# Scaling the normed tokens ahead of the transposition instead of inside it, in a two-layer encoder trunk

## The chip, the core and the metric

The kernel runs on one core of a Trainium2 chip. The metric is the device time of one execution in microseconds (us). The engines named here are TensorE (PE, matrix products; PEld is its weight load), VectorE (DVE), ScalarE (ACT), GpSimd (POOL) and the sync engine's queue of transfers (SP). Each engine works through its own instructions in the order in which they were compiled; semaphores tie the engines together.

## The reference

`x` holds 512 tokens of 1024 features, all F32. Two layers follow, each a token mixer (retention, stick-breaking attention and gated linear attention on one input projection) and a convolutional FFN of width 2816. What matters here is what stands around every sub-layer:

```python
def rmsnorm(x, g):
    xf = x.astype(jnp.float32)
    y = xf * lax.rsqrt(jnp.mean(xf * xf, axis=-1, keepdims=True) + EPS)
    return (y * g.astype(jnp.float32)).astype(x.dtype)
...
        hn = rmsnorm(x, pre_mix_g[l]) * (1.0 + sc1) + sh1
        y = token_mixer(hn, w_in[l], gla_w2[l], gla_b[l], ret_norm_g[l], gla_norm_g[l], w_out[l])
        x = x + g1 * rmsnorm(y, post_mix_g[l])
        hn = rmsnorm(x, pre_ffn_g[l]) * (1.0 + sc2) + sh2
        y = conv_ffn(hn, w_up[l], conv_w[l], conv_b[l], w_down[l])
        x = x + g2 * rmsnorm(y, post_ffn_g[l])
```

So between any two sub-layers a residual is formed, normed, scaled and shifted, and it has to lie transposed (features on the partitions) for the next products.

## The kernel before, in words

The tokens are four blocks of 128, here block 0 to 3 (`tb` in the code). A block of the residual is two tiles of 128x512 F32 (`xt[0]`, `xt[1]`), with the tokens on the partitions. Every large product is done with three products of first and second parts: an operand is cast to a first part (`hi`, `hnh`; ScalarE, lines 352 and 332) and the rest is a second part (`lo`, `hnl`; VectorE, lines 353 and 333). All products of the program are recorded at line 92, and transpositions at line 95.

There are four places at which tokens are normed and transposed. At the start, `start_x` does it for the input. Three hand-overs follow: the first from the mixer to the FFN of layer 0 (about 353 to 390 us in the trace), the second from that FFN to the mixer of layer 1 (724 to 790 us), the third from the mixer to the FFN of layer 1 (1061 to 1100 us). The last FFN writes the output.

In a hand-over each block goes the same way. `close0` and `close1` square the two banks of the sub-layer's output on ScalarE (line 516, junk output, sum kept), multiply it by the gate's row on VectorE (518), and get 1/rms from two small VectorE operations (283, 284) and one on GpSimd (286). The old residual is loaded again by the sync queue (`load_x`), the sum is formed on VectorE (522), stored, squared on ScalarE (298, twice), and 1/rms of the sum is got in the same way. `scaled_ident` then multiplies the identity by it (304). `prenorm_T`, run when `flush` calls it, does four products of 128x128 into each of two PSUM banks, evicts the first bank in four pieces on ScalarE (328) and the second in four on VectorE (330), with the scale and shift of the next sub-layer, and makes the first and second parts (332, 333).

The two banks come from the `pj` pool of three banks. So the second bank of block 1 takes the bank that the first of block 0 had, and waits for its eviction, and the banks of block 2 wait in the same way for those of block 0 and of block 1. In the second hand-over the products of `sv` (lines 502 on, `proj_tok`, evicted at 544) share these banks. An FFN begins with the products of blocks 0 and 1 for four tiles of w_up (the lead products), goes on with those of blocks 2 and 3, and only then to whole rows of tokens.

Nothing orders the work around the change but the program: the compiler's scheduler sets each engine's order when the kernel is built, from the dependences and its own idea of durations. Transfers on the sync queue go in that order too; a load of a weight tile waits until the tile that had its slot has been split into its parts.

## Time and profile before

| | us |
|---|---|
| median of three runs | 1462.37 |
| lowest, highest | 1459.83, 1466.27 |
| profiled execution, span from first to last instruction | 1457.7 |
| PE busy in that span | 1409.9 (97%) |
| DVE, ACT, POOL busy | 832.6 (57%), 661.5 (45%), 36.1 (2%) |
| mean granted clock of TensorE | 0.976 |

The page gives the profiled execution's span alone; no time of its own stands beside it. The median lies 4.67 us above that span. A stretch in which PE is not busy, or runs at less than the full clock, adds to the time unless PE can do other work in it; the other engines have slack on average, but each in its order.

### The profile page before, as it was taken

What the parts mean: (1) busy time and instruction counts of PE and PEld (TensorE: products, weight loads), DVE (VectorE), ACT (ScalarE), POOL (GpSimd) and SP (SyncE); (2) the same over time, 40 slices, a digit from 0 to 9 for tenths busy, and PEclk for the clock granted to TensorE, in tenths of its full rate; (3) what the DMA queues carried; (4) which work ended last, traced back from release to release, by engine and by line L of the source; (5) the groups of instructions that cost most, each with busy time, mean ns of one, the idle gap of its engine ahead of it and who ended that gap; (6) DMA issues with size and microseconds to landing.
All of it is one profiled execution on the core that took longest, in us unless ns stands there. A gap on an engine that the chain in (4) does not pass through costs nothing. (4 is left out here: it accounts for less than half of the span.)

```text
span 1457.7 us, 19702 instructions
## 1 busy us (share of the span) xinstructions
PE 1409.9 (97%) x7619; PEld 1131.1 (78%) x7619; DVE 832.6 (57%) x1544; ACT 661.5 (45%) x1081; POOL 36.1 (2%) x57
## 2 busy tenths in 40 slices
PE   8999799999999999999989999999999999999998
PEld 6887476768878778888879877777789888888886
DVE  4459687655878784433654486576575444443232
ACT  5455366745533333332244565766564333333130
POOL 0000000000000000000010000000010000000000
PEclk9999799989999999999999999999899999999999
DMA  8635272203688772222773221022053222223222
GB/s 308 213 122 151 92 229 73 73 30 127 208 235 255 215 232 101 101 87 101 246 172 112 87 87 59 30 73 73 29 203 102 92 97 102 98 90 101 101 102 101
DMA packets 73614, 186.22 MB, mean 128 GB/s; under 512 B 8448, under 2 KB 9520, under 8 KB 73520
## 3 DMA queue, kind: packets, MB, share of 16 engines
q1 hardware_dynamic: 72512, 182.68, 38.8%
q0 software_dynamic: 704, 2.11, 0.5%
q8 instruction: 60, 0.98, 0.3%
q14 instruction: 34, 0.28, 0.1%
q10 hardware_dynamic: 304, 0.16, 0.0%
HBM read 176.51 MB, written 8.41 MB: 127 GB/s over the span
## 5 line engine op out<-in xcount | busy, mean ns | idle before, releaser
L353 DVE TENSOR_TENSOR lo<-raw,hi 128x1024 fp32r<-128x1024 f32 (+2 forms) x208 | 245.7, 1184 | 259.1 <-ACT hi L352 254.3
L92 PE MATMUL pj<-hnh,hi 128*128 128x512 f32 x976 | 385.8, 395 | 7.5 <-DVE m__867_4559 L914 3.3
L92 PE MATMUL pj<-hnh,lo 128*128 128x512 f32 x976 | 384.4, 394 | 0.0
L92 PE MATMUL pj<-hnl,hi 128*128 128x512 f32 x976 | 383.3, 393 | 0.0
L352 ACT CAST hi<-raw 128x1024 fp32r<-128x1024 f32 (+2 forms) x208 | 211.3, 1018 | 332.3 <-PE pj L92 170.6
L92 PEld LDWEIGHTS pj<-hnh,hi 128*128 128x128 f32 x976 | 184.8, 189 | 48.2 <-issue 8.9
L92 PEld LDWEIGHTS pj<-hnh,lo 128*128 128x128 f32 x976 | 184.5, 189 | 39.5 <-issue 1.1
L92 PEld LDWEIGHTS pj<-hnl,hi 128*128 128x128 f32 x976 | 184.7, 189 | 37.7 <-issue 0.2
L250 DVE SCALAR_TENSOR_TENSOR ada<-ada,cB 128x512 f32<-128x512 f32 x160 | 107.6, 688 | 40.6 <-DMA ada<-ada 40.2
L92 PE MATMUL pj<-hi,hnh 128*128 128x384 f32 (+1 forms) x160 | 52.2, 326 | 5.2 <-ACT m__1248_6605 L544 5.2
L92 PE MATMUL pj<-lo,hnh 128*128 128x384 f32 (+1 forms) x160 | 51.8, 324 | 0.3 <-DVE lo L353 0.3
L92 PE MATMUL pj<-hi,hnl 128*128 128x384 f32 (+1 forms) x160 | 51.7, 323 | 0.0
L286 POOL TENSOR_TENSOR s<-s,nhalf 128x1 f32<-128x1 f32 x32 | 20.0, 625 | 795.2 <-DVE s L284 790.5
L92 PE MATMUL ps<-hnl,hi 128*128 128x256 f32 x128 | 36.4, 288 | 1.1 <-DVE hnl L333 1.1
L92 PE MATMUL ps<-hnh,lo 128*128 128x256 f32 x128 | 36.0, 285 | 0.0
L92 PE MATMUL ps<-hnh,hi 128*128 128x256 f32 x128 | 35.8, 290 | 0.0
L92 PEld LDWEIGHTS pj<-hi,hnh 128*128 128x128 f32 x160 | 30.8, 192 | 5.8 <-ACT m__1248_6605 L544 5.4
L516 ACT ACTIVATE junk<-ps 128x512 bf16<-128x512 f32 x16 | 9.5, 596 | 50.8 <-PE ps L92 50.5
L92 PEld LDWEIGHTS pj<-lo,hnh 128*128 128x128 f32 x160 | 30.8, 192 | 0.9 <-DVE lo L353 0.7
L92 PEld LDWEIGHTS pj<-hi,hnl 128*128 128x128 f32 x160 | 30.7, 192 | 0.0
L92 PEld LDWEIGHTS ps<-hnl,hi 128*128 128x128 f32 x128 | 24.6, 194 | 1.6 <-DVE hnl L333 1.6
L92 PEld LDWEIGHTS ps<-hnh,hi 128*128 128x128 f32 x128 | 24.8, 198 | 0.0
(2770 smaller groups left out, 2536.2 us busy)
## 6 DMA issues: line engine op xcount, KB each, us to landing
raw<-wu SPq DMA_DIRECT2D x88, 512.0 KB, 3.3
ada<-ada SPq DMA_DIRECT2D x160, 256.0 KB, 3.5
raw<-wd SPq DMA_DIRECT2D x44, 512.0 KB, 3.2
raw<-wT SPq DMA_DIRECT2D x42, 512.0 KB, 3.6
raw<-wo SPq DMA_DIRECT2D x16, 512.0 KB, 3.2
raw<-wsv SPq DMA_DIRECT2D x8, 384.0 KB, 4.0
raw<-wrv SPq DMA_DIRECT2D x8, 384.0 KB, 2.9
raw<-wgv SPq DMA_DIRECT2D x8, 272.0 KB, 2.8
```

The costliest lines, as they stand in the source:

```text
L92: self.last = self.e.matmul(*a, **k)
L250: V.scalar_tensor_tensor(raw, raw, 1.0, cB[h], ALU.mult, ALU.mult, accum_out=pt[:, 4 * h + j : 4 * h + j + 1])
L286: G.tensor_tensor(r, v, nhalf, ALU.pow)
L352: SC.copy(h, raw)
L353: V.tensor_tensor(l_, raw, as32(h), ALU.subtract)
L516: SC.activation(junk, ps, AF.Square, accum_out=ss)
```

## The change

The pool of the diagonals and `scaled_ident` go. `scaled` takes their place: half of a block (128x512) is multiplied by 1/rms on VectorE, the other half on ScalarE. At the start it writes in place; in a hand-over it writes to two new tiles, as the unscaled residual is still being stored. TensorE then transposes the scaled tiles with the identity. Comments were taken out too, so that later lines have numbers that are lower by one.

```diff
-    dgp = ctx.enter_context(tc.tile_pool(name="dgp", bufs=2))
...
-    def scaled_ident(r):
-        # a product with the diagonal of 1 / rms both scales and transposes
-        dg = dgp.tile([P, P], F32, tag="dg", name=nm("dg"))
-        V.tensor_scalar(dg, ident, r, None, ALU.mult)
-        return dg
+    def scaled(xt, r, to):
+
+        V.tensor_scalar(to[0], xt[0], r, None, ALU.mult)
+        SC.activation(to[1], xt[1], AF.Copy, scale=r)
+        return to
 
     def prenorm(tb, xt, ft, a, sh, hi, lo):
         r = rstd_of(square_sums(xt))
-        dg = scaled_ident(r)
-        late[tb] = lambda: prenorm_T(tb, xt, dg, ft, a, sh, hi, lo)
+        xn = scaled(xt, r, [T(ft), T(ft)])
+        late[tb] = lambda: prenorm_T(tb, xn, ft, a, sh, hi, lo)
...
-    def prenorm_T(tb, xt, dg, ft, a, sh, hi, lo):
+    def prenorm_T(tb, xn, ft, a, sh, hi, lo):
         for h in range(2):
             ps = psj()
             for j in range(4):
-                PE.matmul(ps[:, j * P : j * P + P], xt[h][:, j * P : j * P + P], dg, start=True, stop=True)
+                PE.transpose(ps[:, j * P : j * P + P], xn[h][:, j * P : j * P + P], ident)
...
     def start_x(tb):
         cs = slice(tb * P, tb * P + P)
-        dg = scaled_ident(rstd_of(square_sums(xt0[tb])))
+        xn = scaled(xt0[tb], rstd_of(square_sums(xt0[tb])), xt0[tb])
         for h in range(2):
             ps = (psz, psj)[h]()
             for j in range(4):
-                PE.matmul(ps[:, j * P : j * P + P], xt0[tb][h][:, j * P : j * P + P], dg, start=True, stop=True)
+                PE.transpose(ps[:, j * P : j * P + P], xn[h][:, j * P : j * P + P], ident)
```

The order of the instructions on ScalarE and VectorE moves in the hand-overs. ScalarE in the third hand-over, before: `m__1780` is block 0's first bank being evicted, `m__1771` and `m__1772` are block 2's residual (its squares), `m__1797` is block 1's first bank and `m__1815` block 2's; the squares of block 3 follow further down.

```order
L328 ACTIVATE m__1780_9393<-pj_1779_9388,mod1sh2_5617,A12_9267 128x128 x4
L352 CAST hi_1804_9498<-raw_1803_9496 128x1024
L332 CAST hnh_1746_9265<-m__1780_9393 128x512
L298 ACTIVATE junk_112,s_1774_9377<-m__1771_9368 128x512
L332 CAST hnh_1746_9265<-m__1782_9405 128x512
L352 CAST hi_1807_9504<-raw_1806_9502 128x1024
L298 ACTIVATE junk_112,s_1775_9378<-m__1772_9369 128x512
L516 ACTIVATE junk_112,s_1784_9437<-ps_1783_9412 128x512
L352 CAST hi_1810_9510<-raw_1809_9508 128x1024
L328 ACTIVATE m__1797_9471<-pj_1796_9466,mod1sh2_5617,A12_9267 128x128 x4
L328 ACTIVATE m__1815_9569<-pj_1814_9564,mod1sh2_5617,A12_9267 128x128
L332 CAST hnh_1746_9265<-m__1797_9471 128x512
```

ScalarE at the same place, after: `m__1778` is block 2's residual, `m__1785` its scaled half, `m__1787` block 0's first bank; `m__1795` and `m__1796` are block 3's residual, `m__1803` its scaled half, `m__1805` block 1's first bank.

```order
L297 ACTIVATE junk_109,s_1781_9395<-m__1778_9386 128x512
L515 ACTIVATE junk_109,s_1791_9456<-ps_1790_9431 128x512
L303 ACTIVATE m__1785_9404<-m__1778_9386,s_1783_9401 128x512
L327 ACTIVATE m__1787_9412<-pj_1786_9407,mod1sh2_5622,A12_9280 128x128 x4
L351 CAST hi_1818_9531<-raw_1817_9529 128x1024
L331 CAST hnh_1750_9278<-m__1787_9412 128x512
L331 CAST hnh_1750_9278<-m__1789_9424 128x512
L351 CAST hi_1839_9801<-raw_1838_9799 128x1024
L297 ACTIVATE junk_109,s_1798_9474<-m__1795_9465 128x512
L297 ACTIVATE junk_109,s_1799_9475<-m__1796_9466 128x512
L303 ACTIVATE m__1803_9484<-m__1796_9466,s_1801_9481 128x512
L327 ACTIVATE m__1805_9492<-pj_1804_9487,mod1sh2_5622,A12_9280 128x128 x4
```

Block 0's eviction moved from ahead of block 2's squares to behind block 2's scaling, and block 1's from ahead of block 3's squares to behind block 3's scaling.

VectorE in the third hand-over, before: `dg_1778` is block 2's diagonal, `m__1799` block 1's second bank, `m__1788` and `m__1789` block 3's residual.

```order
L283 TENSOR_TENSOR s_1776_9381<-s_1774_9377,s_1775_9378 128x1
L284 TENSOR_SCALAR s_1776_9381<-s_1776_9381 128x1
L304 TENSOR_SCALAR dg_1778_9386<-ident_95,s_1777_9384 128x128
L518 TENSOR_TENSOR m__1785_9439<-ps_1783_9412,g1_1_9056 128x512
L283 TENSOR_TENSOR s_1786_9441<-s_1724_9194,s_1784_9437 128x1
L284 TENSOR_SCALAR s_1786_9441<-s_1786_9441 128x1
L353 TENSOR_TENSOR lo_1811_9511<-raw_1809_9508,hi_1810_9510 128x1024
L330 TENSOR_SCALAR m__1799_9483<-pj_1798_9478,A12_9267,mod1sh2_5617 128x128 x3
L522 SCALAR_TENSOR_TENSOR m__1788_9446<-m__1725_9196,s_1787_9444,m__1788_9446 128x512
L333 TENSOR_TENSOR hnl_1747_9266<-m__1797_9471,hnh_1746_9265 128x512
L522 SCALAR_TENSOR_TENSOR m__1789_9447<-m__1785_9439,s_1787_9444,m__1789_9447 128x512
```

VectorE at the same place, after: `m__1787` and `m__1789` are block 0's two banks, `m__1795` and `m__1796` block 3's residual, `m__1802` its scaled half, `m__1807` block 1's second bank.

```order
L517 TENSOR_TENSOR m__1792_9458<-ps_1790_9431,g1_1_9069 128x512
L352 TENSOR_TENSOR lo_1819_9532<-raw_1817_9529,hi_1818_9531 128x1024
L332 TENSOR_TENSOR hnl_1751_9279<-m__1787_9412,hnh_1750_9278 128x512
L332 TENSOR_TENSOR hnl_1751_9279<-m__1789_9424,hnh_1750_9278 128x512
L521 SCALAR_TENSOR_TENSOR m__1795_9465<-m__1729_9209,s_1794_9463,m__1795_9465 128x512
L521 SCALAR_TENSOR_TENSOR m__1796_9466<-m__1792_9458,s_1794_9463,m__1796_9466 128x512
L352 TENSOR_TENSOR lo_1840_9802<-raw_1838_9799,hi_1839_9801 128x1024
L282 TENSOR_TENSOR s_1800_9478<-s_1798_9474,s_1799_9475 128x1
L283 TENSOR_SCALAR s_1800_9478<-s_1800_9478 128x1
L302 TENSOR_SCALAR m__1802_9483<-m__1795_9465,s_1801_9481 128x512
L329 TENSOR_SCALAR m__1807_9504<-pj_1806_9499,A12_9280,mod1sh2_5622 128x128 x4
L332 TENSOR_TENSOR hnl_1751_9279<-m__1805_9492,hnh_1750_9278 128x512
```

Block 0's second parts moved from ahead of block 2's 1/rms to behind its scaling, and block 1's eviction from ahead of block 3's residual to behind block 3's scaling. The first hand-over has the same order on both engines.

ScalarE in the second hand-over, before: `m__1216` is block 0's first bank, `m__1207` and `m__1208` block 2's residual, `m__1232` block 1's first bank.

```order
L328 ACTIVATE m__1216_6448<-pj_1215_6443,mod1sh1_4271,A11_6300 128x128 x4
L332 CAST hnh_1184_6298<-m__1216_6448 128x512
L332 CAST hnh_1184_6298<-m__1218_6460 128x512
L298 ACTIVATE junk_112,s_1210_6432<-m__1207_6423 128x512
L298 ACTIVATE junk_112,s_1211_6433<-m__1208_6424 128x512
L352 CAST hi_1242_6570<-raw_1241_6568 128x768
L352 CAST hi_1245_6576<-raw_1244_6574 128x768
L516 ACTIVATE junk_112,s_1219_6503<-ps_1110_5957 128x512
L328 ACTIVATE m__1232_6537<-pj_1231_6532,mod1sh1_4271,A11_6300 128x128 x4
```

ScalarE there, after: `m__1217` is block 2's scaled half, `m__1219` block 0's first bank, `m__1226` and `m__1227` block 3's residual, `m__1234` its scaled half, `m__1236` block 1's first bank.

```order
L303 ACTIVATE m__1217_6451<-m__1210_6433,s_1215_6448 128x512
L327 ACTIVATE m__1219_6459<-pj_1218_6454,mod1sh1_4276,A11_6305 128x128 x4
L351 CAST hi_1246_6583<-raw_1245_6581 128x768
L331 CAST hnh_1184_6303<-m__1219_6459 128x512
L331 CAST hnh_1184_6303<-m__1221_6471 128x512
L515 ACTIVATE junk_109,s_1222_6514<-ps_1110_5962 128x512
L351 CAST hi_1249_6589<-raw_1248_6587 128x768
L351 CAST hi_1268_6751<-raw_1267_6749 128x1024
L297 ACTIVATE junk_109,s_1229_6532<-m__1226_6523 128x512
L297 ACTIVATE junk_109,s_1230_6533<-m__1227_6524 128x512
L303 ACTIVATE m__1234_6542<-m__1227_6524,s_1232_6539 128x512
L327 ACTIVATE m__1236_6550<-pj_1235_6545,mod1sh1_4276,A11_6305 128x128 x4
```

Here too block 0's eviction went behind block 2's scaling, and block 1's behind block 3's.

## Rows read from the trace of the kernel before

**Rows 1.** Part 1 of the page: busy time of each engine, its share of the span and its instructions.
```profile
PE 1409.9 (97%) x7619; PEld 1131.1 (78%) x7619; DVE 832.6 (57%) x1544; ACT 661.5 (45%) x1081; POOL 36.1 (2%) x57
```

**Rows 2.** The chain of waits over the whole span, its longest pieces in order of time: start, us, engine, tile, line.
```profile
1083.34 3.87 DMA m__1788_9446<-x
...
1088.71 8.54 PE ps L92 x69
```

**Rows 3.** Timeline of TensorE at 742 us, block 0 of the second layer's mixer being transposed between two products of w_down: start, us, line, tiles, shapes, count of records (a product of two F32 operands leaves two records).
```profile
742.15 1.05 PE L92 MATMUL pj<-dg,m__1168_6244 128*128 128x128 f32 x8
743.04 1.06 PE L92 MATMUL pj<-dg,m__1169_6245 128*128 128x128 f32 x8
743.86 0.48 PE L92 MATMUL ps<-m__1141_6153,m__872_4596 128*128 128x512 f32 x1
```

**Rows 4.** Timeline of TensorE at 178 us: a transposition that the kernel before already has (four of 128x128 F32 with the identity, line 95), and the next product.
```profile
177.83 0.60 PE L95 MATMUL ps<-ident,m__331_1727 128*128 128x128 f32 x4
178.27 0.59 PE L92 MATMUL ps<-m__328_1703,blk 128*128 128x512 f32 x1
```

**Rows 5.** Instructions by tile and by line: count, duration in ns (min/median/max), first and last start, forms. The diagonal; a VectorE scaling of 128x512; a ScalarE copy with a scale of 128x512.
```profile
L304 DVE TENSOR_SCALAR dg<-ident,s x16: 276/286/292, 8.9 to 1091.8; 128x128 f32<-128x128 f32 x16
...
L1019 DVE TENSOR_SCALAR m__13_135<-m__13_135,A,mods x1: 548/548/548, 24.1 to 24.1; 128x512 f32<-128x512 f32 x1
...
L423 ACT ACTIVATE m__441_2269<-m__441_2269 x1: 615/615/615, 237.1 to 237.1; 128x512 f32<-128x512 f32 x1
```

**Rows 6.** Timeline of TensorE in the third hand-over (second layer, mixer to conv FFN): the diagonal products of block 2 (one PSUM bank each) and the first product of the conv FFN that is followed by others without a gap (1088.71). In brackets the idle time ahead of it and what ended it.
```profile
1084.15 1.16 PE L92 MATMUL pj<-dg,m__1771_9368 128*128 128x128 f32 x8 [0.96 <-DVE dg L304]
1086.34 1.16 PE L92 MATMUL pj<-dg,m__1772_9369 128*128 128x128 f32 x8 [1.03 <-ACT m__1797_9471 L328]
...
1088.71 0.38 PE L92 MATMUL ps<-hnl,hi 128*128 128x256 f32 x1 [0.74 <-DVE hnl L333]
```

**Rows 7.** Timeline of ScalarE in the same stretch: a cast of a weight tile (352), the evictions of block 1 (328), a cast of a normed tile (332), and the second sum of squares of block 3.
```profile
1079.97 1.04 ACT L352 CAST hi<-raw 128x1024 fp32r<-128x1024 f32 x1
...
1084.78 1.50 ACT L328 ACTIVATE m__1797_9471<-pj,mod1sh,A 128x128 f32<-128x128 f32 x4
...
1086.51 0.63 ACT L332 CAST hnh<-m__1797_9471 128x512 fp32r<-128x512 f32 x1
...
1089.41 0.63 ACT L298 ACTIVATE junk<-m__1789_9447 128x512 bf16<-128x512 f32 x1
```

**Rows 8.** Timelines of VectorE and, last row, GpSimd in the same stretch: a second part of block 0 (line 333) and of a weight tile (353), block 2's diagonal (304), block 3's residual (522).
```profile
1080.46 0.69 DVE L333 TENSOR_TENSOR hnl<-m__1780_9393,hnh 128x512 fp32r<-128x512 f32 x1
...
1081.67 1.22 DVE L353 TENSOR_TENSOR lo<-raw,hi 128x1024 fp32r<-128x1024 f32 x1
...
1083.81 0.29 DVE L304 TENSOR_SCALAR dg<-ident,s 128x128 f32<-128x128 f32 x1 [0.66 <-POOL s L286]
...
1088.57 0.75 DVE L522 SCALAR_TENSOR_TENSOR m__1789_9447<-m__1785_9439,s,m__1789_9447 128x512 f32<-128x512 f32 x1
...
1083.22 0.55 POOL L286 TENSOR_TENSOR s<-s,nhalf 128x1 f32<-128x1 f32 x1 [5.55 <-DVE s L284]
```

**Rows 9.** Timeline of TensorE in the first hand-over (first layer, mixer to conv FFN), the first gapless product at 376.66; and VectorE's diagonal of block 2 there.
```profile
376.66 0.58 PE L92 MATMUL ps<-hnl,hi 128*128 128x256 f32 x1 [0.35 <-DVE hnl L333]
...
371.45 0.28 DVE L304 TENSOR_SCALAR dg<-ident,s 128x128 f32<-128x128 f32 x1 [0.66 <-POOL s L286]
```

**Rows 10.** The second hand-over (conv FFN of the first layer to mixer of the second). TensorE: the first of sv's products for block 0, and for block 1; ScalarE: block 0's eviction, and the copy of sv's block 0; VectorE: block 2's diagonal, two second parts of weights, block 3's residual; then the issue of block 3's reload on the sync queue (count, ns, first and last start).
```profile
753.82 0.42 PE L92 MATMUL pj<-hi,hnh 128*128 128x384 f32 x1
...
766.00 0.69 PE L92 MATMUL pj<-hi,hnh 128*128 128x384 f32 x1 [5.16 <-ACT m__1248_6605 L544]
...
743.25 1.50 ACT L328 ACTIVATE m__1216_6448<-pj,mod1sh,A 128x128 f32<-128x128 f32 x4
...
765.49 0.46 ACT L544 COPY m__1248_6605<-pj 128x384 f32<-128x384 f32 x1
...
755.47 0.28 DVE L304 TENSOR_SCALAR dg<-ident,s 128x128 f32<-128x128 f32 x1 [0.66 <-POOL s L286]
755.67 1.82 DVE L353 TENSOR_TENSOR lo<-raw,hi 128x768 fp32r<-128x768 f32 x2
...
764.01 0.75 DVE L522 SCALAR_TENSOR_TENSOR m__1224_6513<-m__1220_6505,s,m__1224_6513 128x512 f32<-128x512 f32 x1 [1.90 <-DMA m__1224_6513<-x]
...
L174 SPq DMA_DIRECT2D m__1224_6513<-x x1: 424/424/424, 757.5 to 757.5; - x1
```

**Rows 11.** Timeline of TensorE at the start: block 0, block 3 and the products behind them.
```profile
9.21 2.07 PE L92 MATMUL ps<-dg,m__5_118 128*128 128x128 f32 x8 [2.07 <-DVE dg L304]
...
17.27 0.94 PE L92 MATMUL ps<-dg,m__11_130 128*128 128x128 f32 x6 [0.80 <-DVE dg L304]
...
20.75 0.41 PE L92 MATMUL pj<-m__54_267,m__2_105 128*32 128x256 f32 x2
```

**Rows 12.** Busy time by stretch: us, PE, PEld, DVE, ACT and POOL busy (instructions), PEclk as a part of full speed, DMA share, GB/s.
```profile
9.00:13.00 4.00, 3.79 (x19) 3.79 (x20) 1.25 (x6) 2.41 (x9) 1.10 (x2) 0.57 1.05 405
374.00:378.00 4.00, 3.65 (x18) 3.36 (x19) 3.49 (x9) 3.02 (x10) 0.18 (x1) 0.57 0.81 281
766.00:770.00 4.00, 4.00 (x12) 4.00 (x13) 3.27 (x10) 2.41 (x6) 0.55 (x1) 0.50 0.35 107
1084.00:1089.00 5.00, 3.08 (x22) 2.69 (x23) 4.76 (x11) 4.42 (x11) 1.54 (x2) 1.00 1.00 362
```

## The prediction

> **What bounds the kernel now.** I read the page's busy times first: PE is busy for 1409.9 us of a span of 1457.7, 97% [rows 1], so that whatever PE loses is lost, and work added on the other engines counts only where PE waits for it. The chain of waits came second. From 1088.71 us on it is products alone; just before stands the reload of block 3's residual and the third hand-over [rows 2]. The third view was the timeline of the hand-overs, engine by engine, as there the changed lines are all that PE waits for: 0.96 us for a diagonal, 1.03 for an eviction, 0.74 for a second part in the third one [rows 6], and 5.16 us for a copy that stands behind block 3's squares in the second [rows 10]. The reader is to see that PE waits little there now, and for work that three engines pass to and fro in a fixed order.
>
> **What TensorE gains.** Within a dense stream a bank of four diagonal products takes (743.86 - 742.15) / 2 = 0.86 us [rows 3]. Four F32 transpositions with the identity take 178.27 - 177.83 = 0.44 us [rows 4]. That is 0.42 us a bank, 0.83 a block, and 32 x 0.42 = 13.4 us for 16 blocks if all of it were on the path.
>
> **What the scaling costs.** On VectorE 0.55 us takes the place of 0.29, 16 times: 4.2 us. On ScalarE 0.62 us is new, 16 times: 9.8 us [rows 5]. With both engines well under PE's load this costs nothing in itself; what it is worth is decided by what stands behind it in the hand-overs, where ScalarE didn't wait for 1/rms before and now does.
>
> **The third hand-over.** The order shows what counts. ScalarE now evicts block 0 only after it has scaled block 2, and block 1 only after it has scaled block 3; VectorE likewise. Before, block 1 was evicted from 1084.78 on [rows 7], ahead of block 3's squares, and the lead products ran from 1088.71. They need block 1's parts. Now the path is one long string, with durations from [rows 5, 7, 8]:
>
> Block 2's diagonal stood at 1083.81. Its 1/rms no longer has block 0's two second parts ahead of it (1081.67 - 1080.46 = 1.21), and block 0's shorter transposition moves all by up to 0.8, of which I count half: its scaling starts at 1082.2. From there: scaling 0.62, eviction of block 0 1.50, a weight's cast 1.04, its second part 1.22, block 0's two second parts 1.38, block 3's two residual halves 1.50, the second square with the reading of its sum 0.83 (an estimate: 0.63 of the row and 0.2), two small sums with their hand-offs 0.5 (an estimate, as 1083.81 - 1083.22 - 0.55 leaves only hundredths for one), GpSimd 0.55, scaling of block 3 0.62, eviction of block 1 1.50, one more eviction's piece and a cast 0.75 (of which 0.63 is the cast), a second part 0.69: 12.7 us. Successors on one engine start some 0.08 before the record ahead of them ends (755.47 + 0.28 against 755.67 [rows 10]), five times here: 12.3. The lead products start at 1094.5 in place of 1088.71: 5.8 later. PE can't do anything else meanwhile, since its order is nearly the same as before. The transposition of block 3, within the stream, gives back 0.8.
>
> The clock: while PE waited 5.16 us in the second hand-over the clock fell, and 766 to 770 ran at 0.50 of full speed, the 1.2 GHz level: 4 us that would have taken 2 [rows 12, 10]. In 1084 to 1089 it stayed at 1.00, the 2.4 GHz level, as PE had only short waits [rows 12]. With waits of some 8 us it falls here too: +2.0. The third hand-over: 5.8 - 0.8 + 2.0 = +7.0.
>
> **The first hand-over** has the same order. Block 2's diagonal is at 371.45, its scaling so at 369.85, and the lead products at 382.15 in place of 376.66 [rows 9]: +5.5. The clock was already at 0.57 in 374 to 378 [rows 12], which cost up to 1.7 us before; I count 0.7 more. With block 3's 0.8 back: +5.4.
>
> **The second hand-over.** Block 2's diagonal at 755.47 becomes its scaling. Block 0's eviction, at 743.25 before, comes behind: 756.0 to 757.5; a weight's cast (three quarters of 1.04) to 758.3; its second part, 0.91, to 759.1 [rows 10]. This queues further than ScalarE: the sync queue issues the next weight's load only then, and block 3's reload stands behind that load now, its second half at 760.0 instead of 757.5 [rows 10]. The residual that waited for it at 764.01 is at 766.5, and then come 0.75, the square 0.83, sums and GpSimd 1.05, the scaling 0.62, block 1's eviction 1.50, sv's copy 0.46 and a cast 0.62: 772.2. PE went on at 766.00 [rows 10], so +6.2; block 3's transposition gives back 0.8, and the clock is low in both kernels: +5.4.
>
> **The start.** PE waited 2.07 us for the first diagonal and 0.80 for block 3's [rows 11]. The transpositions are shorter, but the scaled halves come later, since ScalarE scales between the squares of the next blocks. By hand the products at 20.75 come 0.4 us sooner; a second fall of the clock would cost up to 2.0 by the stretch at 766. Bounds -0.9 (one block's gain) and +2.0; I take +0.5, nearer the row that shows the clock low in 9 to 13, at 0.57 [rows 12].
>
> **Sum.** 7.0 + 5.4 + 5.4 + 0.5 = +18.3 us. The profiled span of 1457.7 becomes 1476.0; with the 4.67 us by which the median lies above it, 1480.7, rounded to 1481. The bounds of one hand-over: -0.8 at best (the string hides beside other work and only block 3's gain counts), and +9 at worst (the weight's load ahead of block 3's reload takes its time as well, and no overlap of records).
>
> **Rivals.** *The gain comes through.* PE is at 97%, its order hardly moves, and were the waits of the hand-overs to stay as they are, 32 banks give their 0.42 us: -13.4, 1449. For it speaks that every single step moved is short (0.6 to 1.5 us [rows 5, 7]) and that waits in the order need not come true; against it that PE must wait for the eviction of block 1 and that its place behind block 3's scaling is fixed.
>
> *Half and half.* The string in each hand-over is shorter by what I mistook for serial (casts and reloads that run ahead), some 3 us less in each, and block 0's and 1's gains move it forward by 0.8 more: about +1.5 to +2.5 in each and 0 at the start, 1467 and within the bounds of no change for the lower half of it.
>
> *The clock doesn't rise for transpositions.* In a stretch where PE does little else than transpose, the clock would stay at the lower level. Here that is the start: from 13 to 20.75, where the clock is 1.00 now, half of some 6 banks' and the first products' work would be added, about +3, and as much as 1 in each hand-over: 1485 to 1487. The four transpositions at 178 are too short to show it. In the Trainium skill, "TensorE: Matmul & The Clock Gate", Part 4: PE-mode transpose, it says that transpose-mode work doesn't count as busy time for the clock in the way other work does; no stretch of this trace has enough of it to agree or disagree.
>
> *TensorE takes as long as before.* If a transposition of F32 had two passes like a product, nothing would be gained and the hand-overs would cost 18.3 + 3 x 0.8, more at the start: 1486. Rows 4 speak against it ([rows 4] are F32 too).
>
> **Chances.** Forecast (1474 to 1488): 0.58. Clock: 0.10. No gain at all: 0.04. Half and half: 0.16, of which half falls within 0.5% of 1462.37, about 7 us, which is what a measurement of this kernel can tell from no change. The gain: 0.12, of which 0.10 is faster by over 0.5%. So faster 0.10, same 0.15 (with a little of the forecast's lower tail and the gain's upper), slower 0.75. The range reaches from 1460, where the half-and-half case ends, to 1490, the upper bounds of two hand-overs; the forecast's own is 1474 to 1488.
>
> **What would show it.** Right: in the three hand-overs PE idles 5 to 9 us where it idled 1 to 5, ended by ScalarE's line 327 or VectorE's 332; the evictions of block 1 lie behind a scaling of line 303; granted clock near 0.5 after each; transpositions of 0.44 us a bank. Wrong: the lead products start no later than 1088.71, or PE's busy time falls by 13 us with no more idle; or the extra time lies outside the start and the hand-overs.

## The result, and the profile after

The changed kernel takes 1484.93 us in the median of four runs (1479.33 to 1487.62), the kernel before 1461.74 in the same comparison (1459.83 to 1466.27): a ratio of 1.015, with a 95% interval of 1.0118 to 1.0183. It is slower by 23.2 us where 18.3 were forecast; 1484.93 lies inside the range and 4 us above the predicted 1481. The profiled execution took 1486.06 us over a span of 1484.3, so 1.8 us lay around the span; against the span before, 1457.7, it is 26.6 us longer. That is more than the 23.2 us between the medians: with 1.8 us around it, the profiled execution of the kernel before took some 1459.5 us, less than any of the four that were timed here, so the traces compare the changed kernel with a short execution of the kernel before.

The page's first part, after:

```profile
PE 1409.8 (95%) x7491; PEld 1125.9 (76%) x7491; DVE 836.6 (56%) x1544; ACT 671.5 (45%) x1097; POOL 34.9 (2%) x57
```

PE is busy for as long as before, 1409.8 us against 1409.9 [rows 1], though its transpositions cost half. The half is there: a bank takes (755.41 - 755.06) to (755.06 - 754.62), 0.35 to 0.44 us, against 0.86 in [rows 3]. PE's timeline at the same place (start, us, line, tiles, records):

```profile
754.62 0.60 PE L95 MATMUL pj<-ident,m__1190_6316 128*128 128x128 f32 x4
755.06 0.60 PE L95 MATMUL pj<-ident,m__1191_6317 128*128 128x128 f32 x4
755.41 0.48 PE L92 MATMUL ps<-m__1141_6158,m__872_4601 128*128 128x512 f32 x1
```

So the PE work that went came back as the same work at a lower clock (the mean granted clock is 0.958, against 0.976 before), and the time in which PE is idle grew from 1457.7 - 1409.9 = 47.8 to 1484.3 - 1409.8 = 74.5 us, by as much as the span. PE's waits in the three hand-overs, with what ended them in brackets, answer to [rows 6, 9, 10]:

```profile
374.17 1.12 PE L95 MATMUL pj<-ident,m__676_3406 128*128 128x128 f32 x4 [3.37 <-ACT m__692_3470 L327]
...
383.43 1.12 PE L95 MATMUL pj<-ident,m__690_3462 128*128 128x128 f32 x4 [7.30 <-ACT m__710_3550 L327]
384.29 1.01 PE L92 MATMUL ps<-hnh,hi 128*128 128x256 f32 x3
...
769.96 1.11 PE L95 MATMUL pj<-ident,m__1204_6384 128*128 128x128 f32 x4 [5.66 <-ACT m__1219_6459 L327]
...
782.77 0.66 PE L95 MATMUL pj<-ident,m__1216_6450 128*128 128x128 f32 x4 [4.41 <-ACT m__1236_6550 L327]
...
783.81 0.67 PE L92 MATMUL pj<-hi,hnh 128*128 128x384 f32 x1
...
786.83 0.35 PE L92 MATMUL pj<-hi,hnh 128*128 128x384 f32 x1
...
1104.16 1.04 PE L95 MATMUL pj<-ident,m__1771_9348 128*128 128x128 f32 x4 [3.38 <-ACT m__1787_9412 L327]
...
1113.14 1.12 PE L95 MATMUL pj<-ident,m__1785_9404 128*128 128x128 f32 x4 [7.08 <-ACT m__1805_9492 L327]
1113.99 1.01 PE L92 MATMUL ps<-hnh,hi 128*128 128x256 f32 x3
```

The four rows with brackets at 374, 383, 1104 and 1113 us are the first and third hand-over: where PE waited for 0.35 to 1.03 us at a time in [rows 6, 9], and for 1.14 once more in the first, it now waits once for 3.4 us and once for 7.1 to 7.3 us, and what ends these waits, ahead of the second banks of block 1 and of block 2, is ScalarE's eviction (line 327) of block 0 and of block 1. The row behind each second wait is the first gapless product. ScalarE and, in the last three rows, VectorE in the third hand-over show why; they answer to [rows 7, 8] (start, us, engine, line, tiles, in brackets the idle time ahead and what ended it):

```profile
1102.00 0.72 ACT L303 ACTIVATE m__1785_9404<-m__1778_9386,s 128x512 f32<-128x512 f32 x1 [0.42 <-POOL s L285]
1102.62 1.48 ACT L327 ACTIVATE m__1787_9412<-pj,mod1sh,A 128x128 f32<-128x128 f32 x4
1103.99 1.05 ACT L351 CAST hi<-raw 128x1024 fp32r<-128x1024 f32 x1
...
1108.96 0.63 ACT L297 ACTIVATE junk<-m__1796_9466 128x512 bf16<-128x512 f32 x1
...
1110.97 0.72 ACT L303 ACTIVATE m__1803_9484<-m__1796_9466,s 128x512 f32<-128x512 f32 x1 [1.29 <-POOL s L285]
1111.60 1.48 ACT L327 ACTIVATE m__1805_9492<-pj,mod1sh,A 128x128 f32<-128x128 f32 x4
...
1105.08 1.23 DVE L352 TENSOR_TENSOR lo<-raw,hi 128x1024 fp32r<-128x1024 f32 x1 [0.46 <-ACT hi L351]
...
1108.08 0.75 DVE L521 SCALAR_TENSOR_TENSOR m__1796_9466<-m__1792_9458,s,m__1796_9466 128x512 f32<-128x512 f32 x1
...
1109.88 0.15 DVE L282 TENSOR_TENSOR s<-s,s 128x1 f32<-128x1 f32 x1
```

One reads them as one string: scaling of block 2 (303) at 1102.00, eviction of block 0 (327), a weight's cast (351) at 1103.99, that weight's second part (352) at 1105.08, for which VectorE waited for the cast, then, not shown, block 0's two second parts; block 3's residual (521), its second half at 1108.08, the second square (297) at 1108.96, the sums (282) from 1109.88, scaling of block 3 (303) at 1110.97 behind GpSimd's part of 1/rms, eviction of block 1 at 1111.60, and PE's first gapless product at 1113.99. That is 12.0 us; 12.3 were forecast.

To see where the time went I set the same PE instruction of both kernels side by side: block 0's first bank in the first and third hand-over ([rows 3] and the rows at 754 have it for the second), and a product behind block 3's in each. PE's timeline of the kernel before, then of the one after:

```profile
361.48 0.72 PE L92 MATMUL pj<-dg,m__656_3330 128*128 128x128 f32 x5
...
399.95 0.28 PE L92 MATMUL ps<-hnl,hi 128*128 128x256 f32 x1
...
774.03 0.42 PE L92 MATMUL pj<-hi,hnh 128*128 128x384 f32 x1
...
1074.01 1.05 PE L92 MATMUL pj<-dg,m__1743_9256 128*128 128x128 f32 x8
...
1199.99 0.39 PE L92 MATMUL pj<-hnh,lo 128*128 128x512 f32 x1
```

```profile
363.87 0.60 PE L95 MATMUL pj<-ident,m__661_3349 128*128 128x128 f32 x4
...
408.05 0.28 PE L92 MATMUL ps<-hnl,hi 128*128 128x256 f32 x1
...
790.27 0.42 PE L92 MATMUL pj<-hi,hnh 128*128 128x384 f32 x1
...
1093.86 0.60 PE L95 MATMUL pj<-ident,m__1756_9291 128*128 128x128 f32 x4
...
1226.60 0.39 PE L92 MATMUL pj<-hnh,lo 128*128 128x512 f32 x1
```

The changed kernel is late by 2.4 us at the first hand-over, by 8.1 behind it, by 754.62 - 742.15 = 12.5 at the second, by 16.2 behind that, by 19.85 at the third, and by 26.6 at 1226.60, which is also what the span is longer by. So: the start and the first mixer 2.4, the first hand-over 5.7, the FFN of layer 0 4.4, the second hand-over 3.8, the mixer of layer 1 3.6, the third hand-over, with the first tiles of its FFN, 6.8.

One execution of each kernel is compared here, and a second trace shows how far two executions of the same work differ. The tail of transpositions, below, is the kernel before with an addition behind its last product; up to there PE's products are the same in the same order, and yet the one at 1199.99 stands 8.25 us later:

```profile
1208.24 0.39 PE L92 MATMUL pj<-hnh,lo 128*128 128x512 f32 x1
```

Set against the kernel before at the same products, that trace is later by 5.4 us at the first hand-over, and over the three hand-overs by 0.7, -2.2 and 3.0, together 1.5. So the hand-overs' 16.3 us are far outside this, each single figure is good to no more than some 3 us, and the 10.4 us outside the hand-overs stand against 6.8 of the same sort in that trace.

### The profile page after: what moved, and what is told of

Same layout as the page of the kernel before. It is cut to its first block, busy times and chain, and to the rows that moved or that the text cites. A ratio compares the mean times of both kernels' runs of the same rounds, so it can differ in the third digit from the quotient of the medians.

```text
span 1484.3 us, 19453 instructions
## 1 busy us (share of the span) xinstructions
PE 1409.8 (95%) x7491; PEld 1125.9 (76%) x7491; DVE 836.6 (56%) x1544; ACT 671.5 (45%) x1097; POOL 34.9 (2%) x57
## 5 line engine op out<-in xcount | busy, mean ns | idle before, releaser
L92 PEld LDWEIGHTS ps<-hnh,lo 128*128 128x128 f32 x128 | 25.8, 202 | 0.0
```

What stands on the lines that cost most here:

```text
L92: self.last = self.e.matmul(*a, **k)
```

## The experiments

In the runs of the experiments the kernel before took 1458 to 1471 us (medians 1465 to 1468), a little more than in the result above, so they are told by the ratio to it, with its 95% interval. Theory A is the one of the prediction: evictions stand behind the scaling of a later block, and PE waits for them. B, the rival from the prediction, is the clock that wouldn't rise for transpositions. C and D are told where they come in.

**The old product with the new scaling.**

```diff
-                PE.transpose(ps[:, j * P : j * P + P], xn[h][:, j * P : j * P + P], ident)
+                PE.matmul(ps[:, j * P : j * P + P], xn[h][:, j * P : j * P + P], ident, start=True, stop=True)
```

> The changed kernel with one thing undone: the scaled tokens are multiplied by the identity in an ordinary product instead of transposed. ScalarE's order in the hand-overs is the same as in the changed kernel. Theory A (the time was lost because evictions stand behind the scaling of a later block, so PE waits): the waits of 3 to 7 us in the hand-overs stay, each bank costs 0.42 us more, so 1485 to 1495 us. Rival B (transpositions do not hold the clock up, and the cold stretches are what was lost): the cold time goes back from 119 us to near the 65 us of the kernel before, and the time to 1465 to 1475 us.

Measured: 1495.55 us, just above A's range and far from B's, ratio 1.0213 (1.017 to 1.0256). The waits stayed though PE has no transposition left, as the last wait of the first hand-over in PE's timeline shows (7.73 us, 7.30 in the changed kernel). Nor did the time at half clock go back to near 65 us, as B has it: with a mean granted clock of 0.960 over 1494.1 us it is 2 x 0.040 x 1494.1 = 120 us, against 125 in the changed kernel by the same sum (0.958 over 1484.3). With the scaling in place, PE's transposition is worth some 0.6%, the difference of the two ratios (0.1 to 1.2 with both intervals); the scaling and the order that it brings cost 2.1%.

```profile
385.76 1.22 PE L92 MATMUL pj<-ident,m__690_3462 128*128 128x128 f32 x4 [7.73 <-ACT m__710_3550 L327]
```

**The transposition without the scaling.**

```diff
-        V.tensor_scalar(dg, ident, r, None, ALU.mult)
+        V.tensor_scalar(dg, ident, r, 0.0, ALU.mult, ALU.is_gt)
...
-                PE.matmul(ps[:, j * P : j * P + P], xt[h][:, j * P : j * P + P], dg, start=True, stop=True)
+                PE.transpose(ps[:, j * P : j * P + P], xt[h][:, j * P : j * P + P], dg)
```

The comparison with 0 makes the diagonal a plain identity that still waits for 1/rms; the scaling by 1/rms is left out.

> The kernel before with the other half alone: PE transposes, but nothing is scaled. The diagonal's instruction is kept in its place and writes a plain identity (its product with 1/rms, compared with zero), so all orders and waits are those of the kernel before; the scaling by 1/rms is left out of the computation. Theory A: only PE's gain is left, 32 banks at 0.42 us less what is hidden in waits: 1449 to 1455 us, cold time near 65 us. Rival B: the clock falls for longer around the transpositions, cold time 85 us or more, 1462 to 1475 us.

Measured: 1467.39 us, ratio 1.0018 (0.9989 to 1.0046). A missed here, and both figures that B gave came: PE's 13.4 us bring nothing that can be measured, and the time at half clock is 94 us where the kernel before had 70 (0.968 over 1462.0, 0.976 over 1457.7). PE's timeline in the first and third hand-over shows where some 4 us go:

```profile
375.47 1.11 PE L95 MATMUL pj<-dg,m__684_3442 128*128 128x128 f32 x4 [3.35 <-DVE dg L304]
...
1088.64 1.12 PE L95 MATMUL pj<-dg,m__1771_9368 128*128 128x128 f32 x4 [2.98 <-DVE dg L304]
```

The waits for block 2's diagonal were 1.14 and 0.96 us before ([rows 6] has the second) and are 3.35 and 2.98 now. PE reaches them sooner by the shorter banks, and the statistics on the other engines come when they come. The 24 us more at half clock cost up to 12 us where PE has work in them. Whether that is the transpositions' own can't be read here; in the run with the ordinary product, above, which has no transposition in these places, it was as long as in the changed kernel. What a transposition does to the clock by itself is for the tail of transpositions, below.

**The scaling at its own block's transposition.**

```diff
-        xn = scaled(xt, r, [T(ft), T(ft)])
-        late[tb] = lambda: prenorm_T(tb, xn, ft, a, sh, hi, lo)
+        late[tb] = lambda: prenorm_T(tb, scaled(xt, r, [T(ft), T(ft)]), ft, a, sh, hi, lo)
```

> The changed kernel with the scaling traced just ahead of its own block's transpositions instead of right behind the sums of squares. On ScalarE block 0's eviction then stands ahead of block 2's scaling, and block 1's ahead of block 3's. Theory A: the two long waits of each hand-over shrink to 1 to 3 us, and with PE's gain the time is 1450 to 1465 us. Rival B: the clock is as low as in the changed kernel, 1475 us or more. Rival C (ScalarE's extra 10 us of work in the hand-overs is what costs, wherever it stands): 1470 to 1480 us.

Measured: 1474.88 us, ratio 1.007 (1.0048 to 1.0093). Half of the loss goes, less than A had said; the time lies in the range of rival C, the work added on ScalarE, which the run with both halves on VectorE and the one with the evictions first take up below. PE now waits for the scaling of block 1, which was done early before and now stands on VectorE, at 376.78, behind the small sums of block 2 and two second parts of weights, and then, for 2.17 us, for a first part. The profile names the last small sum (line 283), which ended just after the scaling. In the second hand-over PE waits once for 8.72 us. The first wait of the first hand-over:

```profile
377.31 1.12 PE L95 MATMUL pj<-ident,m__703_3533 128*128 128x128 f32 x4 [5.05 <-DVE s L283]
```

**The start alone.** The kernel before with scaling and transposition in `start_x` only.

> The kernel before with the change at the start alone; the hand-overs keep the diagonal. Theory A: about +1 to +2 us at the start (PE waits of 3.0, 1.4 and 3.4 us for the scaling there) and nothing else: 1462 to 1464 us. Rival D (the time lost in the FFN of layer 0 and in the second layer's retention does not come from the hand-overs but from where the start puts the loads): 1465 us or more, with the wait of 6.9 us at about 515 us present.

Measured: 1469.66 us, ratio 1.0032 (1.0002 to 1.0062): some 4.7 us of 1465 at the centre, with 0.3 to 9 in the interval. The time is in rival D's range and above A's, which were both set against 1462; the wait that D names is not there. In the FFN PE waits 4.73 us at 518.53, as much as the last two waits of the kernel before there (1.40 and 3.29), so the start doesn't draw the longer one of the changed kernel behind it. At the start itself PE's longest wait in the changed kernel, and the product that answers to 20.75 in [rows 11], are:

```profile
17.82 0.69 PE L95 MATMUL ps<-ident,m__11_127 128*128 128x128 f32 x2 [3.42 <-DVE m__11_127 L302]
...
22.11 0.46 PE L92 MATMUL pj<-m__51_264,m__2_102 128*32 128x256 f32 x2
```

**A tail of transpositions.**

```diff
+    ps = psj()
+    for seg in (0, 1, 0):
+        for i in range((200, 100)[seg]):
+            with tc.issue_after(PE.last.ins):
+                o = ps[:, i % 4 * P : i % 4 * P + P]
+                if seg:
+                    PE.matmul(o, ident, ident, start=True, stop=True)
+                else:
+                    PE.transpose(o, ident, ident)
+    SC.copy(xT[0], ps)
```

> The kernel before with a tail behind its last product that nothing needs: 200 transpositions of the identity (F32 128x128), 100 ordinary F32 products of the identity with itself, and 200 transpositions again, one after another into one bank, on a TensorE that was at the full clock through 360 us of products. It measures the disputed cost by itself. Theory B (a transposition does not count as work for the clock): the granted clock falls to 0.5 within the first 200, comes back in the products, and falls again. Theory A without B: it stays at 1.0 through all of it, some 0.11 us a transposition and 0.21 us a product.

One execution, 1528.16 us. PE's timeline of the tail, and then two of its windows, the first and last 200 (us, busy of PE, PEld, DVE, ACT, POOL, granted clock, DMA share, GB/s):

```profile
1458.71 21.99 PE L95 MATMUL pj<-ident 128*128 128x128 f32 x200
1480.54 22.50 PE L92 MATMUL pj<-ident 128*128 128x128 f32 x200
```

```profile
1459.00:1480.00 21.00, 21.00 (x195) 21.00 (x193) 2.32 (x5) 0.66 (x2) 0.55 (x1) 1.00 0.07 26
1503.00:1524.00 21.00, 21.00 (x195) 21.00 (x194) 0.00 (x0) 0.00 (x0) 0.00 (x0) 1.00 0.00 1
```

The granted clock is 1.00, the 2.4 GHz level, through 22 us of transpositions alone, twice (the second time in 22.00 us). So transpositions hold the clock up, and B, as this run's expectation puts it, is out. That the clock also rises from the lower level during transpositions wasn't tried by itself; in the kernel it is the run with the ordinary product that speaks against B. 200 transpositions take 21.99 us, 0.110 each; 100 products of the same size (two records each) take 22.50, 0.225 each.

**Busy products in the waits.**

```diff
...
+            n = WAITS[ft == FT[1]].get((tb, h), 0)
+            if n:
+                if tb == 1:
+                    late["wp"] = psz()
+                for _ in range(n):
+                    PE.matmul(late["wp"], C["reset"][:, 0:P], C["reset"], start=True, stop=True)
             ps = psj()
```

> The changed kernel with products that nothing needs (bf16, 128x512, as at the start) in the waits of the three hand-overs: 12 ahead of block 1's second bank and 28 ahead of block 2's in the first and third, 24 and 18 in the second, sized to the waits seen there. If the long waits cost by their length alone, the time is that of the changed kernel, about 1485 us, or a little more. If what the clock loses behind them is a part (cold 13.7 us after the first and third hand-over, 13.6 after the second), the cold time in the hand-overs goes from 41 us to under 15 and the time to 1470 to 1478 us.

Measured: 1486.8 us, ratio 1.0132 (1.0084 to 1.018). The time at half clock did fall, from 125 us to 92 over the span (mean granted clock 0.958 and 0.969), and the time didn't move beyond its interval. PE waits for the same eviction behind its 40 busy products, and goes on no sooner (timeline, then windows over the wait and behind it):

```profile
376.83 5.56 PE L93 MATMUL ps<-reset 128*128 128x512 bf16 x25
385.17 0.66 PE L96 MATMUL pj<-ident,m__690_3462 128*128 128x128 f32 x4 [2.77 <-ACT m__710_3550 L334]
```

```profile
376.00:385.00 9.00, 6.39 (x33) 3.17 (x33) 8.07 (x18) 6.21 (x14) 0.86 (x1) 1.00 0.75 265
385.00:389.00 4.00, 3.83 (x21) 3.84 (x22) 3.80 (x10) 4.00 (x12) 0.00 (x0) 0.59 0.47 152
```

So what went is mostly low clock inside the waits, where it costs nothing. Behind the wait, where the forecast counts it, the clock was low here too, 0.59 in 385 to 389, after PE had stood idle for the last 2.77 us; so this run doesn't test what that part costs. In the changed kernel the first two rows of windows below have PE busy for 6.5 and 6.8 us of 14, at 0.52 and 0.51. The other two rows are for the section that follows.

```profile
374.00:388.00 14.00, 6.54 (x31) 5.99 (x32) 13.05 (x29) 10.19 (x22) 0.86 (x1) 0.52 0.62 215
1104.00:1118.00 14.00, 6.76 (x30) 6.21 (x31) 10.84 (x23) 10.35 (x22) 1.15 (x2) 0.51 0.60 202
1118.00:1122.00 4.00, 4.00 (x36) 4.00 (x35) 0.59 (x1) 0.00 (x0) 0.00 (x0) 1.00 0.00 0
933.00:948.00 15.00, 15.00 (x70) 11.61 (x69) 2.93 (x5) 6.52 (x12) 0.00 (x0) 0.54 0.04 16
```

**Both halves scaled on VectorE.**

```diff
-        SC.activation(to[1], xt[1], AF.Copy, scale=r)
+        V.tensor_scalar(to[1], xt[1], r, None, ALU.mult)
```

> The changed kernel with both halves scaled on VectorE. ScalarE does not wait for 1/rms any more, and evicts block 0 without it; VectorE's eviction of block 1 still stands behind block 3's scaling, and ScalarE's behind block 3's squares. Theory A: the string is shorter by the scaling on ScalarE alone, 0.6 us of 12, so little changes: 1478 to 1486 us. Rival C (ScalarE's added work and its wait are the cost): 1460 to 1470 us.

Measured: 1483.99 us, ratio 1.0127 (1.0075 to 1.0178). ScalarE is free of the scaling and of its wait, and nothing is won, as A says; block 1's eviction still stands behind block 3's squares:

```profile
383.36 1.12 PE L95 MATMUL pj<-ident,m__690_3462 128*128 128x128 f32 x4 [6.92 <-ACT m__710_3550 L327]
```

**Both at once.** Both halves scaled on VectorE, at their own block's transposition: the diffs of those two runs together.

> Scaling traced at its own block's transposition, and both halves on VectorE. Evictions on ScalarE then stand ahead of the later blocks' squares, as in the kernel before, and VectorE evicts block 1 behind block 3's residual but ahead of block 3's scaling. Theory A: shorter waits than with the scaling at the transposition on both engines (1474.9 us): 1465 to 1472 us. Rival C: the same as that, 1472 to 1478 us, as VectorE is now the engine with too much in the hand-overs.

Measured: 1481.6 us, ratio 1.0103 (1.0062 to 1.0143). That lies between the changed kernel and the scaling on both engines at the same place (1.007, 1.0048 to 1.0093), and by the intervals it is clear of neither; A's shorter waits didn't come. PE waits 5.58 us for block 1's scaling, which now stands on VectorE behind block 2's residual, its sums and two second parts of weights, and 4.55 for a first part behind it. Why the first part comes later than with both engines wasn't tried.

```profile
381.10 1.11 PE L95 MATMUL pj<-ident,m__703_3533 128*128 128x128 f32 x4 [5.58 <-DVE m__703_3533 L302]
```

**Evictions first.** One line moved: the transposition and eviction of block `tb - 2` are traced ahead of the scaling of block `tb`.

```diff
-        r = rstd_of(square_sums(xt))
-        xn = scaled(xt, r, [T(ft), T(ft)])
+        ss = square_sums(xt)
+        flush(tb - DLY)
+        xn = scaled(xt, rstd_of(ss), [T(ft), T(ft)])
```

> The changed kernel with one line moved: block 0's transposition and eviction are traced ahead of block 2's scaling, and block 1's ahead of block 3's. The same instructions and the same amount of work on every engine; on ScalarE and VectorE the evictions now stand ahead of the scaling that they stood behind. Theory A: the waits of 3.4 and 7 us in the first and third hand-over and of 5.7 and 4.4 in the second fall to 1 to 3 us each, and the ratio to the kernel before from 1.015 to 1.001 to 1.008, of which the start alone is 0.003. Rival C (the amount of work added in the hand-overs is the cost): waits of other names, ratio 1.010 or more.

Measured: 1474.63 us, ratio 1.0057 (1.0037 to 1.0078). This is the run that A stands on: the same instructions on the same data (7491, 1544 and 1097 on PE, VectorE and ScalarE, as in the changed kernel), another order, and 1.5 - 0.57 = 0.9% of the 1.5% is gone, 0.5 to 1.3 with both intervals. The changed kernel was not run again beside it; each ratio is to the kernel before in its own comparison. The traces agree: at the products that were set side by side above, the three hand-overs are 1.3, 1.1 and 2.1 us later than in the kernel before, together 4.5, where the changed kernel's are 16.3. PE's waits in the first hand-over and, last row, the longest of the second:

```profile
378.81 1.11 PE L95 MATMUL pj<-ident,m__693_3485 128*128 128x128 f32 x4 [3.73 <-DVE m__693_3485 L302]
381.38 1.11 PE L95 MATMUL pj<-ident,m__694_3486 128*128 128x128 f32 x4 [1.45 <-ACT m__706_3541 L328]
...
780.56 0.69 PE L92 MATMUL pj<-hi,hnh 128*128 128x384 f32 x1 [5.82 <-ACT m__1252_6618 L544]
```

The first are ended by the scaling (302), an eviction and, for 0.52 us, a cast, and sum to 5.7 us, against 3.37 + 7.30 = 10.7 in the changed kernel; the third hand-over has 3.42 and 1.45 in the same places. That each would fall to 1 to 3 us, as A had it, is missed: 3.7 and 3.4 us for the scaling stay, and in the second hand-over 5.82 us for the copy of sv, where the kernel before waited 5.16 [rows 10]. The waits have other names, as rival C says, but the time is in A's range and not in C's.

**The same with the old start.** `start_x` as in the kernel before.

> The same hand-overs with the start of the kernel before (product with the scaled diagonal). It is the candidate to beat the kernel before. Theory A with the transposition alone (ratio 1.002) and the start alone (1.003): 0.3% under the run beside it, ratio 0.998 to 1.005. If the gain of 0.42 us a bank comes through once the evictions stand first, the ratio is 0.992 to 0.996.

Measured: 1474.3 us, ratio 1.0054 (1.0029 to 1.0079), a little above A's range at the centre; what the start costs can't be seen here. It doesn't beat the kernel before, and no version tried does.

## Why the prediction was right, and where it wasn't

*The third hand-over*: +7.0 forecast, +6.8 measured. The string of 12.3 us was 12.0, PE's first gapless product came at 1113.99 - 19.85 = 1094.1 in the time of the kernel before, 1094.5 forecast: 5.4 late. The two estimates in the string held: the reading of the sum takes 0.18 us in the trace, and from the small sums at 1109.88 to GpSimd's part at 1110.38 it is 0.50. Up to the scaling of block 3 the string is as told, 1110.97 - 1102.00 = 9.0 us for 9.1 less its overlaps. Its last two terms, a cast and a second part of block 1 (0.75 + 0.69), were not on the path: PE waited for the eviction alone and then transposed block 2's second bank, 0.85 us from 1113.14, which the forecast hadn't. That these nearly make up for each other is luck. The clock behind it stayed at 0.51 up to 1118, and was at 1.00 from there (the windows above, second and third row), where it was at 1.00 before [rows 12]: 4 us that would have taken 2, as forecast. Less block 3's 0.8 that makes 6.6.

*The first*: +5.4 forecast, +5.7 measured, by the same string: the first gapless product at 384.29 - 2.4 = 381.9, 382.15 forecast.

*The second*: +5.4 forecast, +3.8 measured. The sync queue's part came as told: the second half of block 3's reload, behind the load of a weight, is issued at 772.51, which is 760.0 without the 12.5 us by which the kernel was late. What PE waited for at the end was the eviction of block 1, not the copy of sv that stands behind it. The product that started at 766.00 [rows 10] starts at 783.81, which is 771.3, for 772.2 (the terms of that string add up to 772.3). The term that was mis-sized is the clock, counted as equal in both: the low clock behind the wait lasted from 783.81 to 786.83 (where a product takes 0.35 in place of 0.52), 3.0 us, and from 766.00 to 770.33 before. Half of that difference, 0.65, was given back beside block 3's 0.8: 5.3 - 0.8 - 0.65 = 3.85.

*TensorE's gain*: the 0.42 us a bank held (0.110 us a transposition in the tail). That it is not on the path but ahead of waits, I had seen for blocks 0 to 2 and still gave the case in which it comes through 12%; with the transposition alone it gives nothing that can be measured, even where the order is the old one.

*The start*: +0.5 was the step that I sized worst among those named; the product at 20.75 came at 22.11, 1.4 us later, and the start alone measured 0.3%. Part of that may be the execution: in the trace with the tail, whose start is that of the kernel before, the same product comes at 19.29, 1.5 us sooner. My count by hand had it 0.4 us sooner but for the clock; PE waited 3.42 us for block 3's scaling, where it had waited 0.80 for the diagonal [rows 11].

*What I had at nothing*: the FFN of layer 0, 4.4 us, and the mixer of layer 1, 3.6 us, stretches with no changed line. In the FFN PE waits for VectorE, where adaLN's sums (line 254) stand between the pieces of the convolution. The longest wait there in the kernel before, then after:

```profile
514.93 0.77 PE L92 MATMUL pj<-hnh,hi 128*128 128x512 f32 x1 [3.29 <-DVE m__867_4559 L914]
```

```profile
515.42 0.76 PE L92 MATMUL pj<-hnh,hi 128*128 128x512 f32 x1 [6.89 <-DVE mod1sh L254]
```

With the shorter ones (2.83 and 1.40 before, 3.09 after), 7.5 us of waits became 10.0, and the clock was at 0.5 for 6.8 us more. In the mixer 933 to 948 ran at 0.54 (the last of the windows above), with PE busy in all of it, where the kernel before was as low for 3.4 us. A low stretch at this place of the program is in every trace, 3.4 us long in the kernel before and in the one with the tail, and as long as here with the start alone and with the transposition alone (0.54 over 919 to 934 and 920 to 935) and with evictions first (0.54 over 930 to 945). So no step of the change accounts for it by itself, and why it was long here stays open. Nor does the FFN's loss go with the change: at the same products the run with both halves on VectorE, whose hand-overs cost as much, loses nothing there, and the kernel before with the tail 1.5 us. These two stretches are the 8 us that I counted at nothing; the hand-overs, forecast at 17.8 together, measured 16.3. By the sign that the prediction gave, extra time outside the start and the hand-overs speaks against it. In the traces of the other runs the same two stretches cost between 1.0 and 9.8 us together, so this part is poorly known; the mechanism that was forecast is the 16.3.

*The clock rival*: given 10%, with 1485 to 1487; and that TensorE takes as long as before, given 4%, with 1486. The measured 1484.93 is nearer to both than to 1481, so the time alone doesn't choose. The bank of 0.35 to 0.44 us rules out the second. Against the first stand the tail of transpositions, in which the clock did not fall, and the run with the ordinary product, in which the time at half clock stayed. The Trainium skill's "TensorE: Matmul & The Clock Gate", Part 4: PE-mode transpose, says that transposing doesn't count as busy for the clock in the same way as other work; for F32 on this chip the measurement decides, 1.00 through 22 us.

*Half and half*, at 1467, was not what happened: the strings were serial, within 0.4 us of the sum in the first and third hand-over.

*The range*: its upper end, 1490, was given as the upper bounds of two hand-overs; by its own terms that is at most 1480.7 + 2 x (9 - 5.4) = 1488. The measured time lies under either.

What is settled by a run: the order costs 0.9% of the 1.5% (0.5 to 1.3). What is argued only: that the 0.57% left is the scaling itself on the path (0.72 us on ScalarE in place of 0.29 for the diagonal, on a string that each block passes) and the start, whose own run, with an interval from 0.02%, is hardly clear of nothing, and without which the kernel with the evictions first is no faster that can be measured.

## What to carry to other kernels

Halving work on the busiest engine is worth little where that engine then waits for someone else: look at what ends its waits before and after the place that gets shorter. A step that waits for a statistic should not be traced ahead of evictions that don't, since on an engine that works in order everything behind it waits too; here one moved line was worth 0.9% (0.5 to 1.3). A chain over three engines can be summed from the durations of the old trace to within a microsecond (0.3, 0.9 and 0.4 us off in the three hand-overs, with some luck in the last terms), if the compiled order is known. And before a difference of a few microseconds in a stretch that wasn't changed is explained, a second execution of the old kernel should be set beside it: here two differ by 8 us.

## What the runs showed of the hardware

A transposition of 128x128 F32 with the identity takes 0.110 us back to back, against 0.225 for the same product, and keeps the clock at 2.4 GHz, in the tail where it was at 2.4 GHz to begin with. ScalarE's scaling of 128x512 by a value per partition took 0.72 us where 0.62 had been read from a copy with a fixed scale [rows 5]; VectorE's took 0.49 where 0.55 had been read. Part of the time at half clock cost nothing, since it fell where PE waited: 33 us less of it, with busy products in the waits, changed the time by nothing that could be measured. Executions of the same products differ in it: the kernel before with the tail was at a granted clock of 0.57 over 219 to 227 us and over 236 to 244, the one without it at 1.00 throughout 213 to 245.
